# The values' projection copied out of PSUM by ScalarE, and the whole program's order taken from the framework's timeline simulation

## The chip, the cores and the metric

One Trainium2 chip, of which the kernel uses one core. The metric is the time of one execution on the device in microseconds; the median of three runs before the change is 1868.44 us (1864.18 to 1869.16).

## The reference, cut to what matters

Two layers of a diffusion block over 512 latent tokens ("x") and 256 context tokens ("ctx"), width 1024. In each layer a normed and modulated input is projected once; the columns of the projection feed four mixers of 256 channels each. The change touches the first, a gated delta rule.

```python
def gdn_prepare(p, conv_w, a_log, dt_bias, latent):
    qkv = jax.nn.silu(dwconv(p[..., :3 * GROUP], conv_w)).astype(jnp.float32)
    ...
    q, k, v = (split_heads(t) for t in jnp.split(qkv, 3, axis=-1))
    q, k = l2norm(q), l2norm(k)
...
    a_mat = jnp.where(strict, jnp.einsum("bhnid,bhnjd->bhnij", kb, k) * decay, 0.0)
    sol = lax.linalg.triangular_solve(sys, rhs, left_side=True, lower=True, unit_diagonal=True)
    def step(s, inp):
        v_new = u_i - jnp.einsum("bhck,bhkv->bhcv", w_i, s)
        o = jnp.einsum("bhck,bhkv->bhcv", qd, s) + jnp.einsum("bhij,bhjv->bhiv", qk_i, v_new)
        s = s * gl[..., None, None] + jnp.einsum("bhck,bhcv->bhkv", kd, v_new)
...
    yx = jnp.concatenate([gdn_x, sc_x, hy_x, na_x], axis=-1) @ w_out[l]
```

`dwconv` is a convolution of width 3 along the tokens, one filter per channel. The other mixers are a short convolution (`sc`), a long convolution by a DFT (`hy`) and a neighbourhood attention (`na`). After the mixers come the output projection and a squared-ReLU MLP of width 4096. The first layer computes both token streams, the second only the latent one, though its keys and values still take the context.

## The kernel before, in words

Every large product is done in three float32r matmuls (lines 138 to 140: weight high by activation high and low, weight low by activation high). Weights come by DMA into `raw`; ScalarE casts the high half `whi` (line 126), VectorE subtracts to get the low half `wlo` (line 127).

In a layer's mixing part each call of `big` projects one block of 128 columns: 24 matmuls of 512 columns into a PSUM tile `mx` (two buffers) and, where the context is needed, 24 of 256 columns into a tile `mc` (one buffer). There are 26 such blocks in a layer. They are called "projection matmuls" below. What they make is used by chains of small work, in this order of the code: the long convolution (tiles `dps`, `yps`); the delta rule, which takes the token-major keys and queries back to channel-major (`fTps`, line 763), builds 48 triangular systems (`grow`, line 833, and `kk`, lines 842 and 844, finished by VectorE into `UQ`, line 849), inverts them, runs a recurrence over six token blocks in two directions, and then the attention heads (`sc`, lines 1199 and 1200, `pt`, line 1221, `op`, line 1230), one unit per head and block of 128 queries. A unit is: scores on TensorE, bias and row maximum on VectorE, the exponential on ScalarE (line 1213), the division by the row sum (line 1218), four transposes, a ScalarE copy `PT` out of PSUM (line 1223), and the product with the values.

The inversion starts with 60 instructions on VectorE that depend on each other (lines 886 and 888, 32x32 triangles), goes through two transposes (`diagT`, line 897) and then to TensorE (`zp`, line 932, `wp`, lines 941 and 978). The recurrence's last product of a step is `typs` (line 1037).

Projections that nobody waits for yet are independent work. The values' projection (`gdn_values`, name "v" in `gdn_project`), the gate's, the attention's and the short convolution's can run wherever TensorE has nothing else; the code names the values' one behind the inversion. A projection of `gdn_project` leaves PSUM through `dwconv` (line 382 on ScalarE, lines 383 and 385 on VectorE, all three reading PSUM), then Silu on ScalarE (line 644), then transposes `tokps` and a copy to `vtok`.

What sets the order is the framework's scheduler. It takes the traced instructions, their dependencies, their place in the code as a priority, and its own estimate of times, and writes one fixed order for each engine. On the chip an engine takes its instructions in that order and waits for semaphores.

Of the kernel before, what the change touches and what calls it, by code (L numbers as in the profile page):

```python
# [45 lines left out]
class Net:  # L46
# [60 lines left out]
    def psum(self, shape, name="ps"):  # L107
        return self.pg.tile(shape, F32, tag="ps", name=name)
# [523 lines left out]
    def gdn_project(self, l, nm, j0, w_in, hx, segs, psum):  # L632

        nc = self.nc
        t = self.tp.tile([128, NBLK, 4, 64], F32, name=nm + "tok", tag=nm + "tok")
        for fb in range(2):
            ps = self.big(w_in[j0 + fb], hx, segs)
            if l == 0 and nm != "v":
                self.step_mods(GPM)
            cv = self.fc("cv")  # L640
            self.dwconv(ps, l, j0 + fb, cv, segs)
            for off, n in segs:
                r = slice(off, off + n)
                self.last_silu = nc.scalar.activation(cv[:, r], cv[:, r], AF.Silu).ins
                g0, g1 = off // 128, (off + n) // 128
                pt = psum([128, g1 - g0, 128], "tokps")
                for tb in range(g0, g1):
                    nc.tensor.transpose(pt[:, tb - g0, :], cv[:, tb * 128:(tb + 1) * 128], self.c["ident"])
                nc.scalar.copy(t[:, g0:g1, 2 * fb:2 * fb + 2, :], pt.rearrange("p t (h d) -> p t h d", h=2))
        return t  # L650
# [1063 lines left out]
```

## Time and profile before

| | us |
|---|---|
| median of 3 runs | 1868.44 |
| lowest, highest | 1864.18, 1869.16 |
| the profiled execution, its own time | 1861.5 |
| its span, first to last instruction | 1859.7 |
| TensorE busy | 1772.7 (95%) |
| VectorE busy | 1267.8 (68%) |
| ScalarE busy | 774.3 (42%) |

The busy time of TensorE counts a matmul from its start to its modelled end, so that matmuls that follow each other overlap; the step from start to start is what a matmul costs in a dense stretch. The granted clock (PEclk) is the share of 2.4 GHz that TensorE was given; it has two levels, 1.2 and 2.4 GHz, so 0.95 over a stretch means that a tenth of it ran at the lower one.

### The profile page before, as it was taken

What the parts mean: (1) busy time and instruction counts of PE and PEld (TensorE: products, weight loads), DVE (VectorE), ACT (ScalarE), POOL (GpSimd) and SP (SyncE); (2) the same over time, 40 slices, a digit from 0 to 9 for tenths busy, and PEclk for the clock granted to TensorE, in tenths of its full rate; (3) what the DMA queues carried; (4) which work ended last, traced back from release to release, by engine and by line L of the source; (5) the groups of instructions that cost most, each with busy time, mean ns of one, the idle gap of its engine ahead of it and who ended that gap; (6) DMA issues with size and microseconds to landing.
All of it is one profiled execution on the core that took longest, in us unless ns stands there. A gap on an engine that the chain in (4) does not pass through costs nothing. (4 is left out here: it accounts for less than half of the span.)

```text
span 1859.7 us, 29504 instructions
## 1 busy us (share of the span) xinstructions
PE 1772.7 (95%) x11170; PEld 1436.0 (77%) x11170; DVE 1267.8 (68%) x2366; ACT 774.3 (42%) x1548; POOL 263.1 (14%) x273
## 2 busy tenths in 40 slices
PE   6899888999999999999999999988899999999998
PEld 2667777788889888888888866777687787777776
DVE  5889898767776777655555586789756765544545
ACT  6333643466565222212222363463347662332323
POOL 0202531600120000000000041162330110000002
PEclk9999999999999999999999999999999999999999
DMA  8452213353565443433444233212235653322322
GB/s 300 150 182 97 91 63 114 118 147 124 182 212 170 146 129 117 123 124 114 130 125 131 83 141 111 69 60 91 73 103 152 210 182 98 106 98 78 115 80 85
DMA packets 105346, 233.55 MB, mean 126 GB/s; under 512 B 13202, under 2 KB 18132, under 8 KB 103925
## 3 DMA queue, kind: packets, MB, share of 16 engines
q1 hardware_dynamic: 105204, 231.68, 38.4%
q8 instruction: 88, 1.44, 0.3%
q14 instruction: 54, 0.43, 0.1%
HBM read 208.42 MB, written 23.21 MB: 125 GB/s over the span
## 5 line engine op out<-in xcount | busy, mean ns | idle before, releaser
L126 ACT CAST whi<-raw 128x512 fp32r<-128x512 f32 x444 | 273.6, 620 | 666.9 <-PE pb L140 269.8
L127 DVE TENSOR_TENSOR wlo<-raw,whi 128x512 fp32r<-128x512 f32 x444 | 317.1, 720 | 216.2 <-ACT whi L126 210.1
L140 PE MATMUL pb<-acth,wlo 128*128 128x512 f32 (+2 forms) x808 | 282.1, 349 | 0.2 <-DVE wlo L127 0.2
L139 PE MATMUL pb<-actl,whi 128*128 128x512 f32 (+2 forms) x808 | 281.8, 349 | 0.0
L138 PE MATMUL pb<-acth,whi 128*128 128x512 f32 (+2 forms) x808 | 280.9, 348 | 0.0
L138 PE MATMUL pb<-whi,hid 128*128 128x512 f32 x628 | 249.7, 398 | 0.8 <-ACT whi L126 0.6
L139 PE MATMUL pb<-wlo,hid 128*128 128x512 f32 x628 | 248.6, 396 | 0.3 <-DVE wlo L127 0.2
L140 PE MATMUL pb<-whi,hid 128*128 128x512 f32 x628 | 248.7, 396 | 0.0
L1498 DVE TENSOR_TENSOR acc<-acc,pb 128x1024 f32<-128x1024 f32 x96 | 117.2, 1221 | 152.6 <-PE pb L140 151.5
L258 DVE SCALAR_TENSOR_TENSOR junk<-adrow,cbc 128x512 bf16<-128x512 f32 x256 | 181.7, 710 | 6.0 <-DMA adrow<-in_adaD_dram 2.9
L139 PE MATMUL mx<-actl,whi 128*128 128x512 f32 x416 | 172.3, 414 | 1.4 <-POOL actl L374 1.2
L140 PE MATMUL mx<-acth,wlo 128*128 128x512 f32 x416 | 171.7, 413 | 0.5 <-DVE wlo L127 0.4
L138 PE MATMUL mx<-acth,whi 128*128 128x512 f32 x416 | 168.8, 406 | 2.1 <-ACT acth L235 1.2
L138 PEld LDWEIGHTS pb<-acth,whi 128*128 128x128 f32 x808 | 152.1, 188 | 20.4
L140 PEld LDWEIGHTS pb<-acth,wlo 128*128 128x128 f32 x808 | 152.0, 188 | 20.1 <-DVE wlo L127 0.4
L139 PEld LDWEIGHTS pb<-actl,whi 128*128 128x128 f32 x808 | 151.8, 188 | 20.1
L374 POOL TENSOR_TENSOR actl<-et,acth 128x256 fp32r<-128x256 f32 (+2 forms) x64 | 56.2, 896 | 732.7 <-DVE et L373 728.5
L138 PEld LDWEIGHTS pb<-whi,hid 128*128 128x128 f32 x628 | 117.8, 188 | 33.0 <-ACT hid L1399 5.4
L140 PEld LDWEIGHTS pb<-whi,hid 128*128 128x128 f32 x628 | 117.8, 188 | 29.5 <-DVE hid L1400 1.8
L139 PEld LDWEIGHTS pb<-wlo,hid 128*128 128x128 f32 x628 | 117.8, 188 | 28.3 <-DVE wlo L127 1.1
L138 PEld LDWEIGHTS mx<-acth,whi 128*128 128x128 f32 x416 | 79.5, 191 | 19.1 <-ACT acth L235 1.6
L139 PEld LDWEIGHTS mx<-actl,whi 128*128 128x128 f32 x416 | 79.7, 192 | 18.3 <-POOL actl L374 1.9
(398 smaller groups left out, 3015.3 us busy)
## 6 DMA issues: line engine op xcount, KB each, us to landing
raw<-in_w_dram SPq DMA_DIRECT2D x276, 256.0 KB, 2.8
adrow<-in_adaD_dram SPq DMA_DIRECT2D x80, 512.0 KB, 3.7
raw<-in_win_dram SPq DMA_DIRECT2D x104, 256.0 KB, 2.6
raw<-in_wout_dram SPq DMA_DIRECT2D x64, 256.0 KB, 3.0
X<-xdr SPq DMA_DIRECT2D x14, 512.0 KB, 4.4
X<-in_xin_dram SPq DMA_DIRECT2D x12, 512.0 KB, 5.1
xdr<-X SPq DMA_DIRECT2D x10, 512.0 KB, 2.8
adp<-in_adaP_dram SPq DMA_DIRECT2D x16, 256.0 KB, 5.5
```

What stands on the lines that cost most here:

```text
L126: self.nc.scalar.copy(hi, raw)
L127: self.nc.vector.tensor_sub(lo, raw, hi.bitcast(F32))
L138: mmul(o, st[0], mv[0], start=first, stop=False)
L139: mmul(o, st[0], mv[1], start=False, stop=False)
L140: mmul(o, st[1], mv[0], start=False, stop=last)
L258: nc.vector.scalar_tensor_tensor(self.junk, raw[:, hs], 1.0, self.cbc[:, cnd, hs], op0=OP.mult, op1=OP.mult, accum_out=self.part[:, l, cnd ...
L374: nc.gpsimd.tensor_sub(lo[:, r], t, hi[:, r].bitcast(F32))
L1498: op = nc.vector.tensor_add(o, o, ps)
```

## The change

Two edits. For the values alone, each part of the projection is first copied from PSUM to a tile `cvr` in SBUF by ScalarE, and the convolution reads that tile. And the scheduler is told to take its times from a timeline simulation, which changes the order of all engines throughout the program.

```diff
@@ gdn_project
             ps = self.big(w_in[j0 + fb], hx, segs)
             if l == 0 and nm != "v":
                 self.step_mods(GPM)
+            if nm == "v":
+
+                raw = self.fc("cvr")
+                for x, (off, n) in zip(ps, segs):
+                    nc.scalar.copy(raw[:, off:off + n], x)
+                ps = [raw[:, off:off + n] for off, n in segs]
             cv = self.fc("cv")
             self.dwconv(ps, l, j0 + fb, cv, segs)
@@ kernel
-    with tile.TileContext(nc) as tc:
+    with tile.TileContext(nc, schedule_with_timeline_sim=True) as tc:
         Net(tc, aps).run()
```

Lines behind the first edit stand six higher in the changed kernel. The counts of instructions stay the same but for 8 copies and 6 more table loads on ScalarE (27 instead of 21). What moves is where the projection matmuls stand in TensorE's order between five points of a layer's mixing. The number of them between these points, 512 columns wide / 256 columns wide, counted in the two orders:

| | layer 1 before | layer 1 changed | layer 2 before | layer 2 changed |
|---|---|---|---|---|
| ahead of the first fTps | 283 / 276 | 337 / 332 | 283 / 60 | 355 / 120 |
| from there to the last kk | 34 / 36 | 76 / 76 | 29 / 32 | 101 / 48 |
| from there to the first zp | 133 / 132 | 150 / 131 | 164 / 88 | 168 / 24 |
| from there to the last typs | 42 / 39 | 61 / 85 | 51 / 12 | 0 / 0 |
| behind the last typs | 132 / 141 | 0 / 0 | 97 / 0 | 0 / 0 |

The first place is TensorE in the attention heads of the first layer. Before, rows of the heads with projection matmuls (`mx`, `mc`) among them:

```order
L1199 MATMUL sc<-nak,naq 128x256
L1200 MATMUL sc<-nakl,naq 128x256
L140 MATMUL mx<-acth,wlo 128x512
L138 MATMUL mx<-acth,whi 128x512
L1221 MATMUL pt<-cst,P 128x128 x4
L139 MATMUL mx<-actl,whi 128x512
L140 MATMUL mx<-acth,wlo 128x512
L138 MATMUL mx<-acth,whi 128x512
L1221 MATMUL pt<-cst,P 128x128 x4
L1230 MATMUL op<-PT,vk 64x128
L139 MATMUL mx<-actl,whi 128x512
```

The same stretch in the changed kernel:

```order
L1205 MATMUL sc<-nak,naq 128x256
L1206 MATMUL sc<-nakl,naq 128x256
L1227 MATMUL pt<-cst,P 128x128 x8
L1236 MATMUL op<-PT,vk 64x128
L1205 MATMUL sc<-nak,naq 128x256
L1206 MATMUL sc<-nakl,naq 128x256
L1205 MATMUL sc<-nak,naq 128x256
L1206 MATMUL sc<-nakl,naq 128x256
L1236 MATMUL op<-PT,vk 64x128 x7
```

The heads now stand alone; all projection matmuls that stood among them are further up.

The second place is TensorE where the inversion comes back to it in the second layer. Before, the first four `zp` and what follows:

```order
L139 MATMUL mx<-actl,whi 128x512
L932 MATMUL zp<-diagT,UQ 32x32 x4
L140 MATMUL mx<-acth,wlo 128x512
L138 MATMUL mx<-acth,whi 128x512
L139 MATMUL mx<-actl,whi 128x512
```

In the changed kernel the last projection matmul of the layer, and then `zp`:

```order
L140 MATMUL mx<-acth,wlo 128x512
L938 MATMUL zp<-diagT,UQ 32x32 x96
L947 MATMUL wp<-diag,Z 32x32
L951 MATMUL tp<-Z,diag 32x32
L947 MATMUL wp<-diag,Z 32x32 x47
L951 MATMUL tp<-Z,diag 32x32 x23
```

What stood behind `zp`, among the products of the inversion and of the recurrence, is now ahead of it.

The third place is ScalarE in the first layer where the systems' exponentials (`Dm`) begin. Before:

```order
L776 COPY tot<-cum 128x48
L778 ACT_TABLE_LOAD
L778 ACTIVATE eg<-g 128x48
L782 ACTIVATE gl<-tot 128x48
L781 ACTIVATE kds<-kds 128x48
L126 CAST whi<-raw 128x512
L836 ACTIVATE Dm<-grow,lbg 128x128 x24
```

In the changed kernel, with the values' copy, convolution and Silu (lines 644, 382, 650) among them:

```order
L784 ACTIVATE eg<-g 128x48
L788 ACTIVATE gl<-tot 128x48
L126 CAST whi<-raw 128x512
L644 COPY cvr<-mc 128x256
L787 ACTIVATE kds<-kds 128x48
L382 ACTIVATE cv<-cvr,conv 128x256
L655 COPY vtok<-tokps 128x2x128
L650 ACT_TABLE_LOAD
L650 ACTIVATE cv<-cv 128x256
L842 ACT_TABLE_LOAD
L842 ACTIVATE Dm<-grow,lbg 128x128 x8
```

The values' projection is now done ahead of the systems instead of behind them, and its Silu changes ScalarE's table twice between the exponentials.

## Rows read from the trace of the kernel before

**Rows 1.** The page: the span, each engine's busy time, and one row of DMA issues.

```profile
span 1859.7 us, 29504 instructions
...
PE 1772.7 (95%) x11170; PEld 1436.0 (77%) x11170; DVE 1267.8 (68%) x2366; ACT 774.3 (42%) x1548; POOL 263.1 (14%) x273
...
raw<-in_wout_dram SPq DMA_DIRECT2D x64, 256.0 KB, 3.0
```

**Rows 2.** Busy time by stretch, cut at the points of the table above.

```profile
50.00:204.00 154.00, 139.19 (x773) 108.58 (x769) 139.56 (x286) 59.11 (x111) 30.28 (x19) 0.98 0.42 143
204.00:238.00 34.00, 31.37 (x245) 26.69 (x245) 27.43 (x48) 23.04 (x71) 18.28 (x14) 0.95 0.22 75
238.00:297.00 59.00, 50.92 (x278) 44.06 (x277) 55.27 (x90) 19.92 (x34) 18.40 (x12) 0.94 0.23 76
297.00:366.00 69.00, 63.93 (x1267) 53.06 (x1269) 51.68 (x102) 26.17 (x51) 32.44 (x45) 0.95 0.33 108
366.00:458.00 92.00, 91.40 (x703) 75.35 (x698) 64.31 (x165) 64.35 (x149) 6.18 (x11) 1.00 0.51 140
458.00:1056.00 598.00, 595.84 (x2987) 500.97 (x2986) 389.53 (x787) 194.21 (x368) 20.98 (x24) 1.00 0.44 139
1056.00:1217.00 161.00, 148.57 (x745) 113.82 (x744) 118.72 (x182) 76.05 (x149) 41.04 (x36) 0.97 0.29 102
1217.00:1248.00 31.00, 28.06 (x212) 23.47 (x212) 24.18 (x45) 21.37 (x67) 15.59 (x14) 0.94 0.17 61
1248.00:1310.00 62.00, 52.71 (x271) 44.24 (x269) 58.23 (x93) 21.73 (x38) 20.20 (x14) 0.94 0.29 96
1310.00:1371.00 61.00, 58.01 (x1165) 47.15 (x1167) 38.70 (x72) 24.92 (x49) 24.03 (x41) 0.97 0.14 47
1371.00:1430.00 59.00, 57.53 (x459) 45.75 (x460) 40.66 (x90) 41.84 (x94) 6.71 (x11) 1.00 0.57 161
1430.00:1860.00 430.00, 419.27 (x1932) 337.87 (x1930) 234.30 (x342) 170.70 (x314) 24.88 (x24) 1.00 0.36 117
```

Columns: stretch, its length, busy us and instructions of PE, PEld, DVE, ACT, POOL, then PEclk, the DMA share, GB/s.

**Rows 3.** TensorE's waits: us in total, times, longest.

```profile
PE mc L138 <- DVE cv L385: 10.1, 2, 5.2
PE zp L932 <- DVE diagT L897: 7.9, 2, 4.4
```

**Rows 4.** TensorE in order of time, last part of the second layer's heads.

```profile
1411.12 0.40 PE L138 MATMUL mx<-acth,whi 128*128 128x512 f32 x1
...
1411.59 0.28 PE L1199 MATMUL sc<-nak,naq 128*128 128x256 f32 x1
...
1412.54 0.39 PE L140 MATMUL mx<-acth,wlo 128*128 128x512 f32 x1
...
1414.40 0.40 PE L140 MATMUL mx<-acth,wlo 128*128 128x512 f32 x1
...
1428.73 1.09 PE L1230 MATMUL op<-PT,vk 128*64 128x128 f32 x14
```

Columns: start, us to the end, then line, operation, tiles, shape and count.

**Rows 5.** ScalarE's groups in 366 to 458 us, by form: busy us, mean ns.

```profile
L1218 ACT ACTIVATE P<-P,sm 128x512 f32<-128x512 f32 x16 | 11.2, 722 | 0.2 <-DVE sm L1214 0.2
...
L1223 ACT COPY PT<-pt 128x512 f32<-128x512 f32 x16 | 9.4, 587 | 3.2 <-PE pt L1221 3.1
...
L1218 ACT ACTIVATE P<-P,sm 128x256 f32<-128x256 f32 x8 | 4.0, 508 | 1.4 <-DVE sm L1214 1.4
...
L1223 ACT COPY PT<-pt 128x256 f32<-128x256 f32 x8 | 3.0, 371 | 0.9 <-PE pt L1221 0.9
```

**Rows 6.** SyncE's DMA queue in order of time, the heads' loads in the second layer.

```profile
1370.02 0.45 SPq L1164 DMA_DIRECT2D nakl<-nak  x1
...
1376.30 0.59 SPq L1168 DMA_DIRECT2D nak<-nak  x1
```

**Rows 7.** ScalarE in order of time, a table load and the instruction behind it.

```profile
1377.16 1.28 ACT L1096 ACT_TABLE_LOAD   x1
1378.45 0.31 ACT L1096 ACTIVATE ss<-ss,eps 128x16 f32<-128x16 f32 x1
```

## The prediction

> **What bounds the kernel now.** I read the page first: TensorE is busy for 1772.7 of 1859.7 us [rows 1], so the time can only fall where it waits or runs slowly, and rise where it is made to wait. The table of stretches says where that is [rows 2]. From 458 to 1056 us, the first layer's output projection and MLP, it is busy for 595.8 of 598; that part is full, before and after. The stretch from 1430 us on has 10.7 us of idle time around its output projection, which depends on weights arriving and not on what is moved. What is left is the mixing of both layers, 50 to 458 and 1056 to 1430 us. There the idle time (length less busy) is, in the first layer, 14.8, 2.6, 8.1, 5.1 and 0.6 us in the five stretches, in the second 12.4, 2.9, 9.3, 3.0 and 1.5. The granted clock is below 1 in all of them but the last of each layer: 0.95 of 69 us, for example, costs another 3.4.
>
> The reader is to see two things in these rows. The heads' stretches (366 to 458 and 1371 to 1430) hardly wait at all, though they consist of small dependent steps: projection matmuls fill them. And from 238 to 297 and 1248 to 1310 VectorE is the busy one, 55.3 of 59 and 58.2 of 62 us; TensorE waits there for it twice per layer, first at an `mc` tile that the values' convolution has not read yet (10.1 us in two waits), then at `zp` (7.9 in two) [rows 3].
>
> **What the change does, and the price of each part.** The price of a projection matmul is its step: 1411.12 to 1411.59 holds two of 512 columns, 0.235 us each, and 1411.59 to 1412.54 eight of 256 columns, 0.119 each [rows 4]. With the counts of the order, the projections moved cost: in the first layer 19.4 us more ahead of fTps, 14.6 more in the systems, 3.9 more up to zp, 9.9 more up to the last typs, and 47.8 less behind it; in the second 24.1, 18.8, -6.7, -13.4 and -22.8. Each layer's sum is zero; the question is what each stretch makes of its share.
>
> *Ahead of fTps.* Extra work can sink into idle time and clock loss: 14.8 and 0.02 of 154 us, so 17.9, in the first layer; 12.4 and 0.03 of 161, so 17.2, in the second. The bounds are all of it (+1.5 and +6.9) and none (+19.4 and +24.1). In the first layer VectorE is busy for 139.6 of 154 us and TensorE follows it, so I let 15 sink: **+4.4**. In the second VectorE has 42 us free, the idle time is made of single waits, and I let 14 sink: **+10.1**.
>
> *The systems.* Idle and clock hold 4.3 and 4.8 us. The bounds are full use and none. TensorE gets 14.6 and 18.8 us between products that come one after the other on it, and fTps, grow and kk are behind them in its order. I let somewhat over half sink: **+12.1** and **+16.0**.
>
> *Up to zp.* This is VectorE's chain of 60 dependent steps; 3.7 and 3.8 us of it are idle. The values' convolution leaves the stretch, low halves of other weights enter. I take **0** for both. The removed wait at `mc` brings nothing of its own here: without it TensorE reaches zp earlier and waits for `diagT` there instead. The bounds are -3.8 (no idle time of VectorE left) and +3.9 (the projections added in the first layer delay zp after all).
>
> *From zp to the last typs.* In the first layer 9.9 us come in, against 8.5 of idle and clock: +1.4 to +9.9, I take **+6**. In the second all 13.4 go, from a stretch that idles for 3.0: -13.4 if TensorE sets its time, 0 if the chain does. I take **-6**, near the middle, since what remains is pairs of dependent steps.
>
> *The heads alone.* The trace of before contains this case once. In the second layer's last eight units the projections run out at 1414.4, and the units take 18.2 us from the first score at 1411.59 to the end at 1429.8 [rows 4]: 2.28 us each, though TensorE alone could do it faster. In the first layer ScalarE does the division in every unit, not in every second one: half of 0.722 us more, 2.64. The 256-column units cost ScalarE 0.508 + 0.371 where the others cost 0.722 + 0.587, a factor 0.67, so 1.77 [rows 5]. Sixteen and eight of these make 56.4 us; sixteen units of the second layer 36.4. The loads of q and k come first: ten issues from 1370.02 to 1376.9 and 3.0 to land [rows 6, 1], so 8.9 us behind the recurrence, and once more between the two head pairs, 9.9 us of which I count 5.5 as bare (bounds 0 and 9.9). That is 70.8 us instead of 92, **-21.2**, and 50.8 instead of 59, **-8.2**. Of 70.6 us of projections that leave the heads, 29.4 are given back.
>
> *ScalarE.* Eight copies, at most 0.587 each like the `PT` copies out of PSUM, are 4.7 us [rows 5]; six table loads at 1.28 are 7.7 [rows 7]. They hide in ScalarE's idle time: it is busy for 23.0 of 34 us in the systems and 19.9 of 59 behind them [rows 2]. Without that cover, the two loads among each layer's exponentials would put 2.6 us per layer in front of grow and kk. The Trainium skill (ScalarE: Activation LUTs, "What ACT_TABLE_LOAD costs") puts a drain of 1380 ns behind each switch, 2.66 us in all; by that the six would be 16.0 us and the exposed part 5.3 per layer. In this trace the square root behind the load at 1377.16 starts 1.29 us after it [rows 7], so no such drain is seen, and the sum goes by the row.
>
> The sum: first layer 4.4 + 12.1 + 0 + 6 - 21.2 = +1.3; second 10.1 + 16.0 + 0 - 6 - 8.2 = +11.9; together +13.2 us. The profiled execution, 1859.7 in span and 1861.5 in its own time, becomes 1872.9 and 1874.7. It lay 6.9 us below the median of the runs, so the median goes from 1868.4 to **1882 us**, 0.7% slower. A measurement of this kernel tells about 0.3%, 5.6 us, from no change.
>
> **The rivals.**
>
> *The heads follow TensorE (faster).* If the filler-free heads are not paced by the chain but by TensorE's own work, the stretches shrink to 92 - 0.6 - 47.8 = 43.6 and 59 - 1.5 - 22.8 = 34.7 us. The other terms stay at 22.5 and 20.1, so the total is +42.6 - 48.4 - 24.3 = -30.1, or 1838 us. It decides from the point where the two stretches together take less than 108.4 us (151 less 42.6); the forecast has 121.6. For it: the four sc rows of a unit and its transposes can run ahead. Against it: the 18.2 us of the last eight units, with projections for only the first 2.8 of them. A case half way between, at -8 us and 1860, is likelier than the floor.
>
> *No change.* The idle time ahead of the systems takes all it can (6.1 us less than in the sum) and the second loads are covered (11 us less in both layers): -4 us, 1864. It needs no new mechanism, only two of my middle values at their better end.
>
> *The lower clock in the heads (much slower).* The clock fell to 0.94 where TensorE waited 5.0 us or so at one place, and stayed at 1.00 through the heads with their short waits [rows 2, 3]. Alone, the heads have TensorE's own 43.6 of 70.8 us, many short gaps and a bubble of some 5 us between the pairs. If it falls to 1.2 GHz and stays there, the own work doubles to 87.2 and 69.4 us and sets the time: 16.4 and 18.6 more, +48 in all, 1917 us. The Trainium skill (TensorE: Matmul & The Clock Gate, "Why this matters for your kernels") warns that idle gaps between bursts of matmuls bring the array back to the half rate, which is this rival's mechanism. The second half of the heads before, at 1.00 with projections mostly gone, speaks against it for short gaps.
>
> **How the numbers follow.** The forecast, 1872 to 1895 when its middle values are moved by a few us, gets 0.47. The faster rival, 1838 to 1862, gets 0.28: its bound is far but half the way is enough, and my shares of sunk work ahead of fTps are choices. No change gets 0.15, the lower clock 0.10, from 1895 up to 1917. So faster by over 0.3% has 0.28, within 0.3% 0.15, slower 0.57. The range that leaves out a tenth at each end goes from 1850, into the faster rival, to 1903, into the clock's.
>
> **What would show it.** In the changed kernel's profile fTps should come some 4 us later than 204 in the first layer, the last kk some 16 later than 238, zp and the last typs 16 and 22 later, and the first output projection at about 459 instead of 458. Counted from the start of its own mixing, the second layer should have zp 26 us later and the end of the heads 12 later. The heads' stretches should have TensorE idle for 25 us or so, waiting for ScalarE's P and PT, and the wait `mc` for `cv` should be gone. The prediction is wrong if the heads take under 108 us together, if fTps does not move at all, or if the clock row shows long stretches of 0.5 among the heads. It is also wrong if the time moves in the MLP stretches, which I hold fixed.

## The result, and the profile after

The changed kernel takes 1938.8 us (median of four runs, 1936.8 to 1949.6) against 1866.3 of the kernel before on the same chip: 1.040 times as long, with a 95% interval from 1.036 to 1.044. The forecast was 1882, with a range from 1850 to 1903. The direction was right, but the loss is 72 us where the sum of the prediction has 13.

The first two rows of the page of the changed kernel, which answer to [rows 1]:

```profile
span 1935.0 us, 29534 instructions
...
PE 1787.0 (92%) x11170; PEld 1458.8 (75%) x11170; DVE 1280.1 (66%) x2366; ACT 781.8 (40%) x1562; POOL 255.0 (13%) x273
```

Busy time by stretch in the changed kernel, cut at the same points as [rows 2] and with the same columns. The cut at 1056 us lay 13.3 us ahead of the pre-norm at the end of the first layer's MLP; 1105 lies 13.5 ahead of it here.

```profile
50.00:218.50 168.50, 159.58 (x914) 128.37 (x914) 147.35 (x300) 66.65 (x125) 31.28 (x21) 0.99 0.38 130
218.50:272.00 53.50, 50.19 (x336) 43.05 (x337) 34.54 (x55) 34.20 (x92) 13.51 (x12) 1.00 0.16 53
272.00:335.00 63.00, 53.94 (x295) 45.70 (x293) 58.56 (x87) 14.10 (x25) 21.08 (x14) 0.92 0.29 91
335.00:421.50 86.50, 75.39 (x1330) 63.60 (x1330) 57.49 (x126) 29.58 (x55) 32.21 (x43) 0.94 0.26 84
421.50:501.50 80.00, 55.57 (x425) 41.21 (x421) 53.94 (x156) 53.50 (x130) 5.86 (x11) 0.81 0.53 144
501.50:1105.00 603.50, 602.43 (x3029) 509.27 (x3029) 385.87 (x762) 198.26 (x378) 21.04 (x24) 1.00 0.42 134
1105.00:1285.50 180.50, 165.88 (x832) 131.28 (x831) 126.60 (x189) 79.98 (x155) 39.13 (x38) 0.94 0.30 103
1285.50:1332.00 46.50, 46.50 (x317) 39.56 (x315) 29.37 (x55) 34.58 (x90) 15.29 (x15) 1.00 0.27 86
1332.00:1391.00 59.00, 42.94 (x195) 34.20 (x193) 57.34 (x92) 14.42 (x23) 17.12 (x12) 0.92 0.29 96
1391.00:1453.00 62.00, 46.89 (x1124) 41.09 (x1126) 35.62 (x67) 22.52 (x43) 23.48 (x41) 0.83 0.05 16
1453.00:1502.00 49.00, 36.92 (x349) 29.89 (x346) 31.73 (x77) 35.82 (x83) 5.32 (x11) 0.93 0.55 155
1502.00:1935.00 433.00, 415.93 (x1929) 338.91 (x1927) 236.83 (x342) 169.37 (x312) 25.79 (x24) 0.99 0.36 115
```

Set against [rows 2], stretch by stretch, these lengths give the ledger of the change. The terms of the prediction stand beside them:

| stretch | layer 1 predicted | measured | layer 2 predicted | measured |
|---|---|---|---|---|
| up to fTps (layer 2: with the end of the MLP) | +4.4 | +14.5 | +10.1 | +19.5 |
| fTps to the last kk | +12.1 | +19.5 | +16.0 | +15.5 |
| up to zp | 0 | +4.0 | 0 | -3.0 |
| zp to the last typs | +6 | +17.5 | -6 | +1.0 |
| heads | -21.2 | -12.0 | -8.2 | -10.0 |
| output projection and what follows | 0 | +5.5 | 0 | +3.0 |
| sum | +1.3 | +49.0 | +11.9 | +26.0 |

TensorE's longest waits in the changed kernel (us in total, times, longest); [rows 3] are those of before:

```profile
PE zp L938 <- DVE diagT L903: 17.6, 2, 14.5
PE mx L140 <- DVE wlo L127: 13.2, 5, 8.5
PE sc L1205 <- ACT P L1219: 13.2, 12, 5.1
PE sc L1205 <- DMA nak<-nak: 9.1, 5, 2.8
PE nps L365 <- DVE et L373: 8.8, 8, 2.1
...
PE pt L1227 <- ACT P L1224: 5.5, 7, 2.5
...
PE grow L839 <- ACT Dm L842: 3.3, 1, 3.3
```

The wait of `mc` for the values' convolution is gone. In its place the reader sees a wait of 14.5 us for `diagT` in the second layer, where nothing is left to fill VectorE's chain, the heads' waits for ScalarE's `P`, and longer ones at `nps`, the products of the norms (2.6 us in four before), above all in the pre-norm at the end of the MLP. The wait of 3.3 us at `grow` stands in the first layer's systems (there it was 1.6); ScalarE comes late with `Dm` there, as it first waits for the values' convolution:

```profile
239.16 1.28 ACT L650 ACT_TABLE_LOAD   x1 [4.29 <-DVE cv L385]
240.46 0.42 ACT L650 ACTIVATE cv<-cv 128x256 f32<-128x256 f32 x1
240.88 1.28 ACT L842 ACT_TABLE_LOAD   x1
```

The granted clock was 0.94 to 1.00 in [rows 2]; it is 0.81 in the first layer's heads and 0.83 from zp to typs in the second.

### The profile page after: what moved, and what is told of

It reads as the page before. It is cut to its first block, busy times and chain, and to the rows that moved or that the text cites. A ratio compares the mean times of both kernels' runs of the same rounds, so it can differ in the third digit from the quotient of the medians.

```text
span 1935.0 us, 29534 instructions
## 1 busy us (share of the span) xinstructions
PE 1787.0 (92%) x11170; PEld 1458.8 (75%) x11170; DVE 1280.1 (66%) x2366; ACT 781.8 (40%) x1562; POOL 255.0 (13%) x273
## 4 chain that ended last, share of the span: by engine, by line
PE 71%; DVE 11%; DMA 5%; ACT 4%; issue 3%; POOL 0%; SPq 0%; DVEq 0%; ACTq 0%; POOLq 0%
PE pb L139 16%; PE pb L138 16%; PE pb L140 16%; PE mx L138 3%; PE mx L140 3%; PE mx L139 3%; DVE wlo L127 2%; DMA adrow<-in_adaD_dram 1%; DMA raw<-in_w_dram 1%; PE mc L138 1%; PE mc L140 1%; PE mc L139 1%; DVE sys L894 1%; DVE prod L892 1%; DMA raw<-in_wout_dram 1%
## 5 line engine op out<-in xcount | busy, mean ns | idle before, releaser
L138 PE MATMUL pb<-whi,hid 128*128 128x512 f32 x628 | 248.6, 396 | 2.9 <-ACT hid L1405 2.9
L140 PE MATMUL pb<-whi,hid 128*128 128x512 f32 x628 | 241.8, 395 | 0.0
L140 PEld LDWEIGHTS mx<-acth,wlo 128*128 128x128 f32 x416 | 80.2, 193 | 32.9 <-DVE wlo L127 15.7
```

Source lines behind the costliest of these rows:

```text
L138: mmul(o, st[0], mv[0], start=first, stop=False)
L140: mmul(o, st[1], mv[0], start=False, stop=last)
```

## The experiments

The first theory was the prediction's own, with larger sizes: the order pulls the projections ("fillers") out of the gaps of the chains, and the empty gaps cost. Its rivals: the copy costs; the lower clock costs; the timeline order makes the chains themselves worse. The edits below are cut to the lines that matter; a comment behind a line names its run.

**1. The two edits apart.** One kernel has the copy and the old order, the other the order and no copy:

```diff
-    with tile.TileContext(nc, schedule_with_timeline_sim=True) as tc:
+    with tile.TileContext(nc) as tc:          # copy_only
```

> Only the values' copy out of PSUM, the order taken as before (TensorE's order is nearly that of before). Theory A, the order carries the whole loss: the time stays within 8 us of the 1866 of before, TensorE's 10 us of waiting at mc for the convolution shrink, and the wait turns up again at zp. Theory B, the copy itself costs (ScalarE and its tables in front of VectorE's chain): 10 us or more above 1866. Theory C, the copy is a gain which the order hides: 1856 or less.

> Only the order from the timeline simulation, the convolution of the values reads PSUM as before. Theory A: 1930 to 1950, as the changed kernel's 1939, with the same shape (typs some 50 us later, heads some 10 shorter). Theory B: clearly below, 1925 or less, since the copy's part is missing. Theory C: above 1950, since TensorE waits at mc again.

The copy alone: 1869.9 us, 1.003 times as long as before (1.0016 to 1.0044). The order alone: 1945.0, 1.044 (1.041 to 1.047). The order carries the loss. Two of TensorE's waits in the kernel with the copy alone, with the same columns as above:

```profile
PE tokps L654 <- ACT cv L650: 9.5, 2, 5.5
PE zp L938 <- DVE diagT L903: 7.8, 2, 4.5
```

The 10.1 us at `mc` went, as the prediction said, but not to zp: 9.5 us turn up at the transposes `tokps`, which wait for the Silu of the same values. At zp it is 7.8 us, where it was 7.9.

**2. The short convolution back among the heads.**

```diff
-                self.short_conv(l, w_in[20:26], hx, segs, y[2:4])
+                with self.tc.issue_after(self.last_typs):
+                    self.short_conv(l, w_in[20:26], hx, segs, y[2:4])
```

> The changed kernel, with the short convolution's six blocks per layer queued on TensorE behind the last typs, so that they stand among the heads again (144 of 512 and 144 of 256 columns in layer 1, 51 us; 144 of 512 in layer 2, 34 us). Theory A, what matters is where the fillers stand: the stretches ahead of the last typs give back 30 to 50 us in layer 1 and 15 to 30 in layer 2, the heads grow by 12 to 20 and run at a granted clock of 1.00, and the time falls from 1939 to 1885 to 1910; what is left over 1866 is in the output projections and at the end of the MLP. Theory B, the order of the chains themselves is worse: typs moves by less than 15 us and the time stays above 1925.

1954.3 us, 1.049 (1.047 to 1.051): slower still. Stretches of this kernel (kk to zp and zp to typs in layer 1, the same two in layer 2):

```profile
274.80:327.90 53.10, 24.62 (x142) 21.30 (x142) 50.74 (x77) 9.61 (x16) 20.97 (x14) 0.78 0.26 87
327.90:403.80 75.90, 53.50 (x1190) 46.59 (x1192) 51.54 (x114) 24.30 (x45) 30.22 (x43) 0.82 0.20 63
...
1340.40:1389.10 48.70, 8.17 (x50) 6.91 (x46) 46.31 (x75) 5.47 (x8) 16.97 (x12) 0.62 0.15 51
1389.10:1450.60 61.50, 46.37 (x1116) 40.54 (x1118) 35.36 (x66) 22.42 (x43) 23.45 (x41) 0.86 0.05 15
```

The fillers returned to the heads were missing elsewhere, since the order still ran most others ahead of the last kk: from there to zp TensorE is busy for 8.2 of 48.7 us in the second layer. These rows also give the chains with little or nothing among them: kk to zp takes 53.1 us with 67 and 72 projections left (512 and 256 columns wide) and 48.7 with 21 and 24, VectorE being busy for 50.7 and 46.3, and zp to typs 75.9 and 61.5 with no projections at all. The kernel before had 14.5 us of them (42 of 512 and 39 of 256 columns, by the prices of [rows 4]) in a first-layer stretch of 69, and 13.4 in a second-layer one of 61 [rows 2]. So in the second layer the bare chain is no shorter than the filled one of before. In the first it is 7 us longer: there something in the new order other than fillers makes the chain longer.

**3. Every gap filled as before.** All fillers queued behind a point of the chains, so that each stretch but the systems, which get none, holds about the number it held; without and with an edit at the end of the MLP (experiment 6):

```diff
+                        with self.tc.issue_after(self.last_kk):
+                            for _ in range(n - 3):
+                                next(na)
+                            self.gdn_values(l, tok, w_in, hx, full)
+                    with self.tc.issue_after(self.last_kk):
+                        self.gdn_gate(l, w_in[0:8], hx, segs, gdr)
+                        next(na)
+                    with self.tc.issue_after(self.last_kk if l else self.last_zp):
+                        for _ in na:
+                            pass
```

> The changed kernel with every filler queued on TensorE behind a point of the chains, so that each gap holds about what it held before: three attention blocks free, the values, the gate and the next attention block behind the last kk, the last attention blocks (layer 1) or two short-convolution blocks (layer 2) behind the first zp, the short convolution behind the last typs. Theory A, the gaps of the chains have a size of their own and it only matters which of them are left empty: of the idle and slow time that the changed kernel has more than the one before, 79 us in the systems, from zp to typs and in the heads go, and 23 us that it gained ahead of fTps come back; 1875 to 1895. Theory B, the timeline order makes the chains themselves slower: above 1915.

> The two edits of after_fill and after_norm together, if their costs add: 12 to 17 us below after_fill by theory A, so 1858 to 1883; by theory B 1900 or more.

1927.0 us (1.035, 1.032 to 1.037) and 1918.2 (1.030, 1.027 to 1.033). The systems fall to 27.1 and 26.5 us, but theory A failed. Zp to typs in after_fill, layers 1 and 2:

```profile
301.50:383.80 82.30, 66.60 (x1288) 56.42 (x1290) 53.55 (x118) 27.05 (x52) 32.98 (x45) 0.94 0.28 95
...
1358.90:1429.70 70.80, 58.93 (x1164) 49.45 (x1166) 40.23 (x73) 24.81 (x48) 23.67 (x41) 0.85 0.09 30
```

That is longer than before (69 and 61) with about the same fillers (17.0 and 11.3 us, where before has 14.5 and 13.4), and longer in layer 2 than bare. So how many fillers a stretch holds doesn't settle what they cost. The time came out where theory B has it, and for the first layer's bare chain experiment 2 agrees with it; the second layer's is not longer.

**4. Where in the stretch they stand.** Both kernels start from the last one. In the order, its 48 fillers between zp and typs of layer 2 stand in a few runs, of 11, 7 and 21 the longest, all in the inversion; in the kernel before the 63 of this stretch stand in some twenty runs, one of 14 between the fourth and the fifth zp. The first kernel deals them out evenly over the recurrence, the second puts them where the kernel before has them:

```diff
+        groups = [(z[49], 9, z[2:48] + z[50:96]), (z[95], 8, w[:1]), (t[0], 3, w[1:2]), (w[1], 4, w[2:3]),
+                  (w[2], 5, w[3:4]), (w[49], 3, w[50:51]), (w[50], 5, w[51:52]), ...]
+        for prev, n, nexts in groups:
+            for f in todo[:n]:
+                self.tc.add_manual_dep(f, prev.name, dep, reason="place")
```

> The kernel of after_both, whose fillers between the first zp and the last typs (96 projection matmuls in layer 1, 48 in layer 2) stand in a few runs of 7 to 21 in the inversion; here they are dealt out one to five at a time between the products of the recurrence (each queued behind one of them), and the inversion is left bare. Theory A, it is not how many fillers a stretch holds but how finely they stand in its waits: zp to typs falls from 70.6 to 61 to 64 us in layer 2 and from 81.5 to 70 to 77 in layer 1, and the time from 1918 to 1900 to 1907. Theory B, a filler costs its own time in these stretches wherever it stands: within 4 us of after_both.

> The kernel of after_both with the 48 projection matmuls of the second layer between the first zp and the last typs pinned where the kernel before has them: 9 between the fourth and the fifth zp (where TensorE waits for the second diagT), 8 behind the last of these zp, then 3, 4, 5, 3, 5 and so on between single wp, and one each between the typs of the two directions. Theory A, fillers are free only at the products behind which TensorE waits, up to the length of that wait: zp to typs falls from 70.6 to 61 to 64 us in layer 2, as long as with no fillers at all (61.5), the granted clock there rises, and the time falls by 6 to 10 us from after_both's 1918. Theory B, the order of VectorE and ScalarE in this stretch makes it long: 67 to 71 us, no change in time.

Zp to typs of layer 2, in runs (after_both), dealt out evenly (after_spread) and in the places of before (after_place):

```profile
1351.30:1421.90 70.60, 58.93 (x1164) 48.90 (x1166) 40.26 (x73) 24.83 (x48) 23.61 (x41) 0.86 0.09 29
```

```profile
1355.50:1425.10 69.60, 57.84 (x1161) 46.96 (x1163) 37.16 (x69) 24.25 (x47) 24.18 (x41) 0.87 0.09 28
```

```profile
1354.80:1419.50 64.70, 57.19 (x1164) 46.08 (x1166) 40.15 (x73) 24.32 (x48) 24.42 (x41) 0.95 0.11 33
```

Against 61.5 bare (60.9 to 61.6 in five kernels that hold none there, 63.1 in flag_only, 64.2 with the dummies of experiment 7), the same 48 matmuls (11.3 us) cost 9.1 us in runs, 8.1 dealt out evenly and 3.2 in the places of before. Even spreading only moved the loss: the inversion, from the first zp to the first typs, fell from 36.3 to 26.5 us, and the recurrence rose from 34.3 to 43.1. The reading that fits is that a filler is cheap where TensorE waits behind the product it follows (for the second `diagT`, for a `Z`), and no longer than that wait. The granted clock differs too, 0.86 and 0.95, and has a part in it:

```profile
1361.50:1366.50 5.00, 5.00 (x14) 3.49 (x12) 4.50 (x6) 0.79 (x2) 0.00 (x0) 0.50 0.00 0
```

This is the run of 11 in after_both, behind the zp: 5.0 us at 1.2 GHz, where 11 at 0.235 are 2.6. With the run of 7 behind it (2.1 us for 1.6) up to 2.9 of the 5.9 us between runs and places may be the clock. The first 9 of after_place ran at 1.2 GHz as well, 4.1 us, but nearly all inside the wait.

The total moved by less than the runs tell: after_spread 1923.3 (1.032, 1.029 to 1.034), after_place 1920.4 (1.030, 1.028 to 1.033), 2.3 us above after_both. The profiled span of after_place is 6.3 us below after_both's, but that profile is of after_both's slowest run; the gain is shown for the stretch alone.

The same in the heads, over after_spread, by the place of each score and transpose:

```diff
+                n = 96 if l else 288
+                self.late = [heads[i * len(heads) // n] for i in range(n)]
                 self.short_conv(l, w_in[20:26], hx, segs, y[2:4])
```

> after_spread, and the short convolution's fillers dealt out in the same way among the heads' scores and transposes (288 in layer 1, 96 in layer 2) instead of up to 35 in a run. Theory A: the heads, from the last typs to the last op, fall from 101.2 to 88 to 94 us in layer 1 and from 62.8 to 58 to 60 in layer 2, and the time by another 8 to 16 us. Theory B: no change against after_spread within 4 us.

1944.4 us (1.043, 1.041 to 1.046), worse. The first layer's heads in this kernel:

```profile
391.50:505.50 114.00, 98.28 (x714) 80.47 (x709) 66.05 (x169) 64.60 (x149) 6.38 (x11) 0.93 0.41 116
```

114.0 us, against 104.0 with the same fillers in longer runs. Four or five were queued behind each score and each group of transposes; in the order that came out they stand in 41 runs of up to 25 between the last typs and the last op, in after_spread in 28 of up to 40. That such fillers delay the units, whether TensorE would wait there or not, is argued from this.

**5. The heads alone, and work ahead of fTps, in the old order.** First the heads alone: in the kernel before, the short convolution is traced first and the scores are queued behind it.

```diff
-                self.na_heads(l, nad, y[6:8], p, pn, with_ctx)
+                self.short_conv(l, w_in[20:26], hx, segs, y[2:4])
+                with self.tc.issue_after(self.last_big):
+                    self.na_heads(l, nad, y[6:8], p, pn, with_ctx)
```

> The kernel before with the short convolution traced ahead of the heads and the heads' scores queued behind its last matmul: the heads stand alone, in the order of the default scheduler, and the fillers run as a block ahead of them. Heads alone as I took them in the prediction (70.8 and 50.8 us with their loads) or as the changed kernel has them (78.6 and 48.4 from the last typs): from typs to the last op 110 to 128 us in layer 1 and 68 to 74 in layer 2, 1890 to 1915 in all. If the heads alone are paced by TensorE: 95 to 105 and 58 to 64, within 15 us of the kernel before.

1903.3 us, 1.021 (1.018 to 1.024). From the last typs to the output projection, layers 1 and 2:

```profile
373.20:494.30 121.10, 101.98 (x699) 81.53 (x695) 75.91 (x198) 65.74 (x149) 6.66 (x11) 0.92 0.44 128
...
1407.00:1476.30 69.30, 60.80 (x456) 47.75 (x451) 41.96 (x92) 44.09 (x96) 6.36 (x11) 0.98 0.48 136
```

92 and 59 us became 121.1 and 69.3, with the same work: 39 us for fillers that stand ahead of the heads instead of among them. From the first score to the last op the bare heads take 68.8 and 43.5 us here, 71.1 and 41.3 in the changed kernel, where the prediction had 61.9 and 41.9 (its 70.8 and 50.8 less the first loads). In the first layer the same stretch of the kernel before takes 75.5 us with 35.6 us of projections in it, at a granted clock of 1.00: in their places of before they cost 4 to 7 us. In after_both 43.0 us of them make it 90.7.

Then work ahead of the second layer's fTps, with one edge more in the kernel before:

```diff
+            self.tc.add_manual_dep(self.first_fT, self.mark["na", 2].name, ...)   # before_pull
+            self.tc.add_manual_dep(self.first_fT, self.mark["v", 0].name, ...)    # before_pull1
```

> The kernel before with one edge more in the second layer: the first fTps is queued behind the third attention projection, so that 29 projection matmuls of 512 and 36 of 256 columns (11.1 us) run ahead of fTps instead of behind it, 24 of 512 fewer in the heads and 15/20 fewer in the systems. My step for work ahead of fTps (14 us of it sink into idle time there): the stretch from dps to fTps keeps its 92.8 us, the systems and the heads give 2 to 4 us each, and the time falls by 3 to 7 us. Rival: work ahead of fTps costs its own time: 4 to 10 us slower.

> The same with the edge one block later (the values' first block): 53 of 512 and 60 of 256 columns, 19.6 us, ahead of fTps, 62 of 512 (14.6 us) fewer behind the last typs. By my steps 14 of the 19.6 sink and 5.6 stay, the heads give 5 us (8.2 for 22.8 in the prediction), the systems 1 to 2: within 4 us of the kernel before. By the changed kernel's profile (12 us sunk, the heads 10 shorter): 2 to 5 us faster. Rival, own time: 10 or more slower.

The stretches to fTps, to the last kk, and the heads, for the first and for the second of these kernels (93, 31 and 59 us before, the first of them from the first `dps`):

```profile
1126.30:1225.50 99.20, 96.18 (x509) 75.26 (x510) 70.91 (x118) 40.50 (x74) 20.75 (x13) 0.97 0.29 100
1225.50:1246.80 21.30, 20.74 (x182) 17.36 (x180) 15.05 (x29) 18.52 (x63) 12.07 (x12) 1.00 0.17 57
...
1371.90:1430.00 58.10, 52.62 (x430) 41.74 (x427) 37.34 (x85) 40.22 (x91) 6.57 (x11) 1.00 0.55 153
```

```profile
1126.40:1233.60 107.20, 103.24 (x556) 81.83 (x557) 74.19 (x123) 42.69 (x78) 20.78 (x13) 0.98 0.31 106
1233.60:1259.10 25.50, 24.66 (x200) 20.13 (x199) 16.80 (x31) 24.47 (x71) 12.21 (x12) 1.00 0.03 11
...
1382.00:1438.20 56.20, 48.06 (x392) 38.41 (x389) 34.12 (x80) 38.30 (x86) 6.10 (x11) 0.91 0.54 146
```

Of 11.1 us added ahead of fTps 6.2 show, of 19.6 us 14.2: some 5 us sink, not 14. In the changed kernel the same stretch holds 12.7 us more than before and takes the same 93, so what sinks there depends on what else the order moves. The systems give back 9.7 and 5.5 us, the heads 0.9 and 2.8 for 5.6 and 14.6 us of fillers less. In all 1862.1 us, 0.999 (0.997 to 1.000), no difference that can be told, and 1869.7, 1.004 (1.002 to 1.005), slower.

**6. The end of the first layer's MLP.** The kernel before lays its last down-projections between the 8 pre-norm steps of the first token pair; the changed kernel does them ahead and runs these steps bare. One kernel undoes this in the new order, one does it in the old:

```diff
+    late = self.nps.get((1, 0, 0, (1, 1, 2, 3, 3, 4)[h * nf + i] + (t == 5) * 3)) if t > 3 else None
+    with self.tc.issue_after(late) if late else ExitStack():          # after_norm
+    self.tc.add_manual_dep(self.nps[1, 0, 0, 1, 0], self.last_big.name, ...)   # before_bare
```

> The changed kernel with the last two token blocks' down-projections of the first layer's MLP (36 matmuls, 8.5 us) queued in threes between the 8 pre-norm steps of the first token pair, where the kernel before has them. Theory A, the bare pre-norm steps cost the 16.5 us of idle time that this end of the MLP has more than before: 1921 to 1928. Theory B, the pre-norm steps are paced by VectorE and ScalarE at some 2 us each with or without fillers, and only the 8.5 us move: 1928 to 1934. Theory C, no gain: 1935 or more.

> The kernel before with one edge more: the second pre-norm step of the first token pair at the end of the first layer's MLP is queued behind the last down-projection, as the changed kernel has it, so that the steps run bare and the down-projections are done ahead of them. Theory A, the bare steps and the lower clock they bring cost what the changed kernel loses there: 8 to 16 us more in all, 1874 to 1882, with a stretch of lower clock behind the pre-norm. Theory B, the loss in the changed kernel comes from the order of the projections behind them: within 4 us of the kernel before.

From the first pre-norm step to the first `dps`, in the kernel before, the changed one, after_norm and before_bare:

```profile
1069.00:1124.00 55.00, 48.73 (x239) 36.12 (x238) 47.02 (x70) 31.83 (x65) 24.41 (x26) 1.00 0.35 126
```

```profile
1118.00:1192.00 74.00, 60.37 (x280) 46.04 (x279) 47.16 (x68) 32.95 (x65) 22.52 (x26) 0.86 0.25 86
```

```profile
1116.70:1193.70 77.00, 67.45 (x303) 50.80 (x302) 49.86 (x74) 34.63 (x70) 24.56 (x26) 0.87 0.28 96
```

```profile
1074.80:1136.70 61.90, 52.55 (x239) 39.76 (x238) 46.81 (x69) 33.02 (x64) 21.33 (x26) 0.91 0.32 111
```

This stretch lost 19 us. Bare steps cost 7 in the old order, with the same work in the stretch (1874.6 us, 1.004, 1.003 to 1.006): the eight steps take 25.7 us instead of 18.2. Undoing them in the new order gave nothing by itself: 1939.8, 1.041 (1.038 to 1.044). With after_fill, the same edit came with 8.8 us less. The counts of the changed kernel say where its 19 us lie. Its eight steps take 19.5 us, with 38 down-projections (8.9 us) fewer among them. The other 18 us lie behind the eighth step, where it has 48 projection matmuls (11.3 us) and 32 small products `abps` (2.0 us) more, brought forward from the mixing. Some 5 us of these 18 stay open; the clock, 0.89 there for 1.00, may be a part.

**7. The clock.** Dummy matmuls that nobody reads: four behind each score of the first layer's heads, and 52 in the wait ahead of the second layer's zp.

```diff
+    with self.tc.issue_after(self.last_score):                                   # after_warm
+        for _ in range(4):
+            nc.tensor.matmul(warm, q, ks[sub][:, 0:512], start=True, stop=True)
+    with self.tc.issue_after(self.last_big):                                     # after_zpwarm
+        for _ in range(52):
+            op = nc.tensor.matmul(warm, x[:, 0:128], x[:, 0:512], start=True, stop=True)
```

> The changed kernel with four more matmuls of 512 columns behind each score of the first layer's heads, whose result nobody reads (192 x... 96 in all, 22.6 us of TensorE at full clock), and the short convolution traced ahead of the heads, so that TensorE has work in its waits. Theory A, the lower granted clock (0.81 in these 80 us) costs time: the clock goes to 0.95 or more and the heads take 68 to 76 us in spite of the added work. Theory B, the chain over VectorE and ScalarE sets the heads' pace and the clock is only its shadow: the clock rises too, but the heads take 78 to 86 us.

> The changed kernel with 52 matmuls of 512 columns whose result nobody reads (12.1 us at full clock), in TensorE's order between the last projection of the second layer and the first zp, where TensorE waits 14.5 us for diagT. Nothing else waits there for TensorE, and the order up to zp is otherwise the same. Theory A, the lower clock that follows a long wait costs time: the granted clock at zp is 1.00, the 192 zp take some 4 us instead of 9, and the last typs comes 5 to 10 us earlier, counted from the first zp 52 to 57 us instead of 61.5. Theory B, the chain over VectorE and ScalarE sets the pace of the inversion whatever the clock: zp to typs stays at 60 to 62 us and the time at 1939.

The wait ahead of zp and the stretch from zp to the first wp, in the changed kernel and in after_zpwarm:

```profile
1377.00:1391.20 14.20, 0.00 (x0) 0.00 (x0) 13.47 (x28) 0.18 (x1) 0.00 (x0) 0.67 0.14 48
1391.30:1401.20 9.90, 3.72 (x196) 3.21 (x197) 5.82 (x4) 3.92 (x6) 1.46 (x2) 0.50 0.01 3
```

```profile
1378.00:1392.60 14.60, 11.93 (x56) 9.57 (x56) 13.86 (x29) 0.51 (x1) 0.00 (x0) 1.00 0.17 54
1392.60:1402.50 9.90, 3.30 (x196) 2.97 (x196) 5.85 (x5) 3.90 (x6) 1.46 (x2) 0.66 0.01 2
```

The clock went from 0.67 to 1.00 ahead of zp and from 0.50 to 0.66 behind it, and the first wp comes 9.3 us behind the first zp in both: TensorE works for under 4 us of these ten, the rest is `diagT` and `Z`. Zp to typs took 64.2 us instead of 61.5, the rest behind the first wp and not explained, and the kernel 1950.5 (1.044, 1.042 to 1.046). The heads of the first layer in after_warm:

```profile
426.80:522.80 96.00, 73.75 (x520) 55.57 (x515) 57.81 (x158) 54.86 (x132) 6.00 (x11) 0.91 0.45 121
```

Their clock rose from 0.81 to 0.91, but they took 96.0 us instead of 80.0 for 22.6 us of dummies (1957.3, 1.050, 1.048 to 1.053). Neither run bore the clock out as the cause where chains set the pace; after_warm can't exclude it, since its dummies stand in the way too.

It does cost where TensorE is full. TensorE's order from fTps to the last kk is the same in the changed kernel and in after_norm. The changed kernel took 53.5 us there at 1.00 (its second row above), after_norm this:

```profile
216.70:275.00 58.30, 55.00 (x337) 47.40 (x338) 34.18 (x55) 34.45 (x92) 13.50 (x12) 0.91 0.15 50
```

4.8 us more, with 10.5 us of it at 1.2 GHz (twice 0.09 of 58.3). Four more kernels have this order there: 53.7 us at 1.00 (after_zpwarm), 55.3 at 0.97 (after_sc3), 58.3 at 0.91 (after_hold and after_warm).

**8. A third score buffer** for the first layer's heads.

```diff
-                    if not with_ctx and unit % 3 == 0:
+                    if unit % 3 == 0:
                         sc = self.pm.tile([128, nk], F32, tag="mc", name="sc", bufs=self.mbufs[1])
```

> The changed kernel with a third PSUM buffer for the scores of the first layer's heads (every third score in the bank of mc, which is idle there, as the second layer does), and the short convolution traced ahead of the heads for that. Theory A, the filler-free heads are held by score buffers that ScalarE has not read yet (10 us of TensorE's waits there): the first layer's heads, 71 us from the first score to the last op, shrink by 4 to 9 us. Theory B, ScalarE and VectorE themselves (53.5 and 53.9 us busy in 80) and the loads set the pace: 2 us or less.

1945.4 us (1.043, 1.040 to 1.045); from the first score to the last op 72.1 us instead of 71.1. The buffers are not what holds the bare heads.

## Why the prediction was wrong

**What held.** The order carries the change, the copy next to nothing. The heads of the second layer (-10.0 for -8.2), its systems (+15.5 for +16.0) and the stretches up to zp were about right. For the systems that is luck, since the same share missed in the first layer (+19.5 for +12.1). The wait at `mc` brought nothing, as forecast, but it moved to `tokps` and not to zp. The rival that heads follow TensorE was refuted: the two stretches take 129 us (it needed under 108.4), and heads alone cost 39 us in the old order too.

**The step that failed first** is the one behind three terms, "extra work can sink into idle time and clock loss": I read a stretch's idle time as room for fillers. In the first layer 19.4 us went in ahead of fTps and 14.5 came out: some 5 sank where I let 15. Some 5 also sank in the second layer's stretch of experiment 5, in the old order, where I let 14. In the first layer's systems nothing sank: 14.6 us went in, 19.5 came out, with a wait for `Dm` of 3.3 us (1.6 before) behind the values' convolution, its Silu and two of the table loads that the prediction let hide. From zp to typs 9.9 went in and 17.5 came out. Experiment 4 shows why the sum of idle time is the wrong measure: the same 48 matmuls cost 3.2 to 9.1 us in one stretch, by their places, though the clock may hold up to 2.9 of that. The three first-layer terms were mis-sized by 29 us together (51.5 against 22.5). That the long runs in the first layer's inversion, 108 fillers where before has 50, act in the same way is argued from these runs; it was not tried apart.

Nor are all of the 17.5 us fillers: 7 of them are the bare chain, which takes 75.9 us in this order against 69 with fillers before (experiment 2). In the recurrence of after_hold VectorE has 20 modulation instructions (line 258, 0.8 us each), 14 in the kernel before, and TensorE's `typs` wait 6.4 us for VectorE's `Y` instead of 1.1; that this is the cause was not tried, and the clock (0.82 against 0.95) is the rival.

**The second** is "from zp to the last typs ... I take -6" in the second layer. The bare chain takes 61.5 us, so what left had been free: the bound of 0 that I named and did not take. Worth 7 us.

**The third** is the price of the heads alone in the first layer, 2.64 us per unit by ScalarE's share: 71.1 us measured from score to op instead of 61.9, and 9 us of the miss. The second layer's price, read off the trace, held (41.3 for 41.9); the one carried over to the first layer did not. The clock, 0.81 there, may be part of it; after_warm does not separate it. What holds these units stays open beyond the score buffers, which it is not.

**The fourth** is the second layer's "I let 14 sink" ahead of fTps: +19.5 for +10.1. I read that stretch as mixing, but it begins in the end of the MLP, among "the MLP stretches, which I hold fixed". Of the 24.1 us of projections 11.3 stand there, ahead of the first `dps`, and that part lost 19 us: the bare pre-norm steps are a part (7 us in the old order), the projections themselves another, some 5 us are open (experiment 6). The other 12.7 us stand between the first `dps` and fTps and nearly all sank, since both kernels take 93 us there (2.0 us of `abps` left that part). In sum nothing did: 24.1 us of projections went in, 8.9 of down-projections left, and the way from the first pre-norm step to fTps is 19.7 us longer. The small plus in 458 to 1056 is that work brought forward: 38 down-projections more lie ahead of the pre-norm.

The rival of a lower clock came true as a mechanism, with 120 us at 1.2 GHz (1935 us at a mean of 0.969, so twice 0.031 of it) instead of 52, but mostly in stretches that a chain paces. The Trainium skill (TensorE: Matmul & The Clock Gate, "Why this matters for your kernels") says that idle gaps bring the half rate back; the rows of experiment 7 agree (0.67 in the wait, 0.50 behind it), and show that this need not cost.

## What to carry to other kernels

Idle time in a stretch is not by itself room for independent work: ask behind which product the engine waits, for how long, and whether a filler would stand exactly there. A long run of fillers, or an even spread, cost most of its own time here. An order from another time model changed nearly every stretch, those held fixed too, so bound those before trusting a sum of small terms.

## What the runs showed of the hardware

Two kernels with one TensorE order in the systems differed there by 4.8 us in 54 through the granted clock alone, 1.00 against 0.91, in a stretch where TensorE is full, and four more kernels with that order fall in line (53.7 us at 1.00, 55.3 at 0.97, 58.3 twice at 0.91); a chain of small products took the same 9.3 us at 0.50 and at 0.66. A table load takes 1.28 us on ScalarE, and in 19 of the 21 of the kernel before the next instruction there starts 11 or 12 ns behind it.
